# Hybrid RG-LRU and neighbourhood-attention block on one core: the second half's q and k are transposed by VectorE and fetched on ScalarE's queue, and the score maxima are ordered ahead of the gate banks

## The chip, the core and the metric

The kernel runs on one core of a Trainium2 chip. Its engines are TensorE (PE in the profile: matmuls, and PEld: their weight loads), VectorE (DVE), ScalarE (ACT), GpSimd (POOL) and SyncE (SP, which here only issues DMAs). Each engine works through its own list of instructions in a fixed order, and an instruction at the head of that list that waits holds up all that stand behind it. The metric is the device time of one execution in microseconds, the median of several runs.

## What is computed

One layer of a hybrid encoder on 512 tokens (a grid of 8 rows by 64 columns) of width 1024, in float32:

```python
x = x + 0.5 * swiglu1(rmsnorm(x))
h = rmsnorm(x)
xr, gr, q, k, v, ga, gb = split(h @ w_in)
xc = depthwise_conv(xr)
y_lru = (rglru_forward(xc) + rglru_backward(xc)) * gelu(gr)
q = rmsnorm(q, q_norm) * 64 ** -0.5          # per head, 16 heads of 64
k = rmsnorm(k, k_norm)
y_att = neighbourhood_attention(q, k, v, rel_pos_bias)
y = sigmoid(ga) * y_lru + sigmoid(gb) * y_att
x = x + y @ w_out
x = x + 0.5 * swiglu2(rmsnorm(x))
```

The attention window of a block of 16 columns is 8 rows by 32 columns, with a softmax over 256 (at the edges 192) keys and a learned bias.

## The kernel before

**Matmuls in three products.** A float32 weight tile `wraw` (128x1024, loaded by SP) is split into a rounded part `wh` and a rest `wl`: a cast on ScalarE (L138; for half of the gate and recurrence weights on VectorE, L140) and then a subtraction on VectorE (L141). Each k tile gives three matmuls into one PSUM bank: `xh*wh` (L166), `xl*wh` (L167), `xh*wl` (L168). The pool holds 3 `wraw`, 4 `wh` and 4 `wl`. So the split of a weight tile can be written only when the tile four chunks earlier has been read for the last time: `wh` after that chunk's last L167, `wl` after its last L168, which is its last matmul.

**Stages.** FFN1 comes first, then the projection `xr` with convolution and recurrence, then q, k and v in two halves of 8 heads, then the gate projections, then `w_out` and FFN2. A gate chunk is 24 matmuls of 128x512 (8 k tiles by 3) into one of the 4 `acc` banks; VectorE evicts it with a multiplication by the reciprocal norm (L1173), and ScalarE applies gelu or tanh to two chunks at once (L1177). VectorE then multiplies the result into the recurrence output A (L1187, L1190).

**Attention between the gate chunks.** Attention runs as a generator `heads()` (L991) in the lane "att". `weave` is called in the middle and at the end of each gate chunk, adds the lane's rate (0.7 in this phase) to its due count, and takes as many steps as are due; so the number of `yield`s decides between which gate chunks a step's matmuls stand. The second half handles four feature tiles (two heads each), numbered `fi` = 0 to 3 here. Its steps are:

- normalize q and k in place (L1004, VectorE),
- `start(fi)` (L1009): 8 transposes on PE (L1013 for q, L1015 for k) into two `aux` banks, then `qh` (ScalarE L1019), `ql` (VectorE L1021), `kh` (ScalarE L1022), `kl` (VectorE L1024). `start(0)` has its own step, `start(1)` to `start(3)` follow the scores before them,
- `scores(fi)` (L1028): 24 matmuls (L1045) into two `aux` and two `acc` banks, the first of which reads `kl`; then, for each of four banks, two reductions `so`/`nmx` on VectorE (L1065: bias added and maximum found, after which the bank is free), two `Exp` on ScalarE (L1072), a reciprocal (L1074) and two scalings on VectorE (L1077),
- `ship(fi)`: the probabilities are transposed on VectorE (L1086, L1087), written to DRAM by SP and fetched by GpSimd as `PT`,
- `apply(fi)`: 32 matmuls with v (L1108) two units later.

**What sets the order.** Within each engine a scheduler sorts the instructions at build time by its own estimate of when each can start; `tc.high_priority()` puts an instruction ahead of others that are ready, `after(i, prev)` forces an order, and `hold(i)` puts an instruction behind the last matmul issued so far. On the chip the order is fixed.

In what follows the gate chunks around the second half's scores are named by their place. In the changed kernel scores(0) stands between chunks 7 and 8, scores(1) between 9 and 10, scores(2) within chunk 11 and scores(3) between 12 and 13. Chunk 7 fills bank `acc_5425`, chunk 8 `acc_5594`, chunk 9 `acc_5626`, chunk 10 `acc_5759`, chunk 12 `acc_5975`.

## Time and profile before

| what | value |
|---|---|
| median of 3 runs | 1082.92 us (1082.89 to 1083.47) |
| profiled execution | 1082.5 us, of which the span is 1080.7 us |
| stage | us from the span's start |
| FFN1 | 0 to 344 |
| xr, convolution, recurrence | 344 to 395 |
| q, k, v in two halves, first gate work | 395 to 546 |
| gate chunks with attention | 546 to 705 |
| w_out | 705 to 752 |
| FFN2 | 752 to 1081 |

In the rows of groups, `out<-in` are the program's tile names; then come the count, the busy time and the mean duration of one in ns, and last the idle time of the engine just ahead of these instructions with what ended it. Rows of a timeline hold the start, the duration, the engine, the line and what is written from what; the durations of neighbours on one engine overlap a little, so a step is read from start to start.

### The profile page before, as it was taken

The numbers are of one execution on the slowest core, as the hardware profiler recorded it, in microseconds if no ns is written. First come the engines' busy times: TensorE is split into PE (matmuls) and PEld (weight loads), VectorE is DVE, ScalarE is ACT, GpSimd is POOL, SyncE is SP. The second block draws the span as 40 slices with busy tenths as digits, with TensorE's granted clock in tenths as the row PEclk, the third lists the DMA queues.
The fourth block names the chain that finished last, engine by engine and source line by source line (L and its number), as shares of the span: only waits on it lengthen the run. The fifth ranks groups of instructions, "written<-read, shape, count | busy, mean of one in ns | idle before, by whom it ended". The sixth has DMA issues, their size and how long they took to land.

```text
span 1080.7 us, 14413 instructions
## 1 busy us (share of the span) xinstructions
PE 1075.3 (99%) x5121; PEld 883.1 (82%) x5121; DVE 770.5 (71%) x1222; ACT 561.6 (52%) x867; POOL 197.8 (18%) x340
## 2 busy tenths in 40 slices
PE   9999999999999999999999999999999999999998
PEld 7888888888888778788877888888888888888887
DVE  7799778774327876999868986758687787764322
ACT  8755555553215778877354642456455555543320
POOL 0110002431000441330345232000001001332000
PEclk9999999999999999999999999999999999999999
DMA  9879675974324685573777576665476777676222
GB/s 356 182 228 246 180 192 135 248 250 148 98 83 146 194 231 155 169 212 104 229 235 219 170 242 205 192 223 160 97 188 188 187 210 167 184 241 198 93 71 79
DMA packets 67464, 198.18 MB, mean 183 GB/s; under 512 B 11072, under 2 KB 12864, under 8 KB 67392
## 3 DMA queue, kind: packets, MB, share of 16 engines
q1 hardware_dynamic: 46736, 136.66, 37.6%
q0 software_dynamic: 20512, 60.34, 25.0%
q8 instruction: 40, 0.66, 0.2%
q14 instruction: 32, 0.26, 0.1%
q10 hardware_dynamic: 144, 0.26, 0.1%
HBM read 162.06 MB, written 26.74 MB: 175 GB/s over the span
## 4 chain that ended last, share of the span: by engine, by line
PE 96%; DVE 2%; DMA 1%; ACT 1%; issue 0%; SPq 0%; ACTq 0%; DVEq 0%
PE acc L318 20%; PE aux L318 15%; PE acc L166 10%; PE acc L168 10%; PE acc L167 10%; PE acc L926 4%; PE acc L927 4%; PE acc L928 4%; PE aux L168 4%; PE aux L166 4%; PE aux L167 4%; PE aux L493 2%; PE aux L1108 1%; PE aux L837 1%; DMA vd<-v 1%; PE aux L1045 1%
## 5 line engine op out<-in xcount | busy, mean ns | idle before, releaser
L141 DVE TENSOR_TENSOR wl<-wraw,wh 128x1024 fp32r<-128x1024 f32 (+2 forms) x147 | 168.9, 1150 | 153.4 <-ACT wh L138 153.0
L138 ACT ACTIVATE wh<-wraw 128x1024 fp32r<-128x1024 f32 (+2 forms) x135 | 134.5, 998 | 224.6 <-PE acc L167 158.2
L141 DVE TENSOR_TENSOR wl<-pair,wh 128x1024 fp32r<-128x1024 f32 x80 | 97.6, 1223 | 42.2 <-ACT wh L138 41.9
L138 ACT ACTIVATE wh<-pair 128x1024 fp32r<-128x1024 f32 x80 | 84.7, 1061 | 77.5 <-PE aux L318 47.8
L166 PE MATMUL acc<-xh,wh 128*128 128x512 f32 x288 | 114.0, 396 | 0.0
L168 PE MATMUL acc<-xh,wl 128*128 128x512 f32 x288 | 112.6, 391 | 0.0
L167 PE MATMUL acc<-xl,wh 128*128 128x512 f32 x288 | 112.5, 391 | 0.0
L318 PE MATMUL aux<-wh,s 128*128 128x512 f32 x320 | 98.5, 389 | 0.0
L318 PE MATMUL acc<-wh,s 128*128 128x512 f32 x320 | 98.5, 389 | 0.0
L926 PE MATMUL acc<-wh,xh 128*128 128x512 f32 x192 | 75.7, 394 | 0.0
L927 PE MATMUL acc<-wh,xl 128*128 128x512 f32 x192 | 74.8, 389 | 0.0
L928 PE MATMUL acc<-wl,xh 128*128 128x512 f32 x192 | 74.7, 389 | 0.0
L318 PEld LDWEIGHTS acc<-wh,s 128*128 128x128 f32 x320 | 60.1, 188 | 12.5
L318 PEld LDWEIGHTS aux<-wh,s 128*128 128x128 f32 x320 | 60.1, 188 | 12.5
L167 PE MATMUL aux<-hl,wh 128*128 128x512 f32 (+1 forms) x179 | 69.3, 387 | 0.0
L168 PE MATMUL aux<-hh,wl 128*128 128x512 f32 (+1 forms) x179 | 69.3, 387 | 0.0
L166 PE MATMUL aux<-hh,wh 128*128 128x512 f32 (+1 forms) x179 | 69.0, 387 | 0.0
L168 PE MATMUL acc<-hh,wl 128*128 128x512 f32 (+1 forms) x176 | 68.1, 387 | 0.0
L167 PE MATMUL acc<-hl,wh 128*128 128x512 f32 (+1 forms) x176 | 68.1, 387 | 0.0
L166 PE MATMUL acc<-hh,wh 128*128 128x512 f32 (+1 forms) x176 | 68.0, 387 | 0.0
L166 PEld LDWEIGHTS acc<-xh,wh 128*128 128x128 f32 x288 | 54.1, 188 | 13.0 <-issue 2.3
L168 PEld LDWEIGHTS acc<-xh,wl 128*128 128x128 f32 x288 | 54.1, 188 | 11.5 <-issue 0.4
(230 smaller groups left out, 2412.3 us busy)
## 6 DMA issues: line engine op xcount, KB each, us to landing
wraw<-wqkv SPq DMA_DIRECT2D x24, 512.0 KB, 4.7
...
```

The source lines that it names most:

```text
L138: mark["H"] = nc.scalar.activation(H, raw, AF.Copy)
L141: mark["L"] = nc.vector.tensor_tensor(L, raw, H.bitcast(F32), ALU.subtract)
L166: nc.tensor.matmul(ps, wh, xh, start=first, stop=False, skip_group_check=skip)
L167: nc.tensor.matmul(ps, wh, xl, start=False, stop=False, skip_group_check=skip)
L168: mark["mm"] = nc.tensor.matmul(ps, wl, xh, start=False, stop=last, skip_group_check=skip)
L318: mark["mm"] = nc.tensor.matmul(pss[tb], x_[:, s], w_[:, c], start=first and k == 0 and x_ is xh_ and w_ is H, stop=k == 3 and w_ is L, sk ...
L493: mark["mm"] = nc.tensor.matmul(pre[tb], x_[:, tb * P : (tb + 1) * P], w_, start=k == 0 and x_ is xh[k] and w_ is H, stop=k == KT - 1 and ...
L837: prev, mm = mm, nc.tensor.matmul(ps[d][b], W[w][o, c], X[x][o], start=x == 1, stop=w + x == 0)
L926: nc.tensor.matmul(pss[j], xh[kk][:, tj], H[:, s], start=kk == 0, stop=False)
L927: nc.tensor.matmul(pss[j], xl[kk][:, tj], H[:, s], start=False, stop=False)
L928: mark["mm"] = nc.tensor.matmul(pss[j], xh[kk][:, tj], L[:, s], start=False, stop=kk == KT - 1)
L1045: mm = hold(nc.tensor.matmul(ps[hp][:, cs], q_[o, n * P : (n + 1) * P], keys(k_[o]), start=k_ is kl, stop=q_ is ql))
```

## The change

Six things are changed, most of them in the attention's second half.

1. The 32 transposes of q and k on PE in the second half go. Instead 8 VectorE transposes (32x32 blocks, one for q and one for k in each of four token blocks) write 128x1024 tiles `pair`, 4 DMAs of 512 KB on SP's queue bring these to DRAM (`qd`), and 4 DMAs per feature tile on ScalarE's queue (`fetch`, 16 in all) fetch them as `xqk`, of which there is one buffer. `qh`, `ql`, `kh` and `kl` then read `xqk` in SBUF instead of PSUM banks. Normalizing is now a generator of its own in a lane "prep"; the factor `k_norm` is folded into q's factor `gq8`.
2. In the second half the scaling of the probabilities (16 instructions on 128x256 and 16 on 128x192) moves from VectorE to ScalarE.
3. All gate weights are cast on ScalarE; before, 12 of the 24 were cast on VectorE.
4. The eviction of a gate chunk is ordered after the last score reduction written so far (`after(e, mark["so"])`).
5. The bias tiles are loaded earlier and with priority.
6. There is one more step ahead of the second half's first scores, and the fetches of later tiles stand in the loop. Buffers are moved about to make room (`big` has 40 instead of 42).

Shown as diff, each hunk without its outer context:

```diff
@@ -78,8 +78,8 @@
     "t0": {"att": 0.0, "lru": 3.25},
-    "t1": {"att": 0.75, "tail": 0.75, "lru": 2},
-    "g": {"att": 0.7, "tail": 0.7, "lru": 1.5, "v": 0.5},
+    "t1": {"att": 0.75, "tail": 0.75, "lru": 2, "prep": 1.0},
+    "g": {"att": 0.7, "tail": 0.7, "lru": 1.5, "v": 0.5, "prep": 1.0},
 }
@@ -104,7 +104,7 @@
 
-    NBIG = 42
+    NBIG = 40
@@ -658,8 +658,8 @@
 
-    lanes = {"att": [], "tail": [], "lru": [], "v": []}
-    due = {"att": 0.0, "tail": 0.0, "lru": 0.0, "v": 0.0}
+    lanes = {"att": [], "tail": [], "lru": [], "v": [], "prep": []}
+    due = {"att": 0.0, "tail": 0.0, "lru": 0.0, "v": 0.0, "prep": 0.0}
@@ -773,7 +773,7 @@
     after(nc.vector.tensor_scalar(gq8, small[:, C_QN : C_QN + 1], HD**-0.5, None, ALU.mult), mark["h"])
-    gk = small[:, C_KN : C_KN + 1]
+    nc.vector.tensor_tensor(gq8, gq8, small[:, C_KN : C_KN + 1], ALU.mult)
@@ -857,7 +857,10 @@
             hold(nc.vector.tensor_tensor(ix, ix, xc[f], ALU.mult))
-            th = big_t(n="th")
+            if d == 1 and f < 3:
+                th = big.tile([P, T], F32, name=nm("th"), **(dict(tag="xqk", bufs=1) if f == 0 else dict(tag="PT", bufs=5)))
+            else:
+                th = big_t(n="th")
             act("tanh", nc.scalar.activation(th, r, AF.Tanh, scale=sp4[:, f * 2 + d : f * 2 + d + 1]))
@@ -938,7 +941,7 @@
         for j, t in enumerate(raws):
-            sq = big_t(n="sq")
+            sq = big.tile([P, T], F32, tag="pt", bufs=2, name=nm("sq"))
             after(nc.scalar.activation(sq, t, AF.Square), copy)
@@ -984,11 +987,12 @@
             bms[g, hp] = tiny.tile([P, 640], F32, tag="bm", bufs=4, name=nm("bm"))
-            ld = nc.gpsimd.dma_start(bms[g, hp], a["rpb"][g * 2 + hp])
+            with tc.high_priority():
+                ld = nc.gpsimd.dma_start(bms[g, hp], a["rpb"][g * 2 + hp])
             if g == 0:
                 after(ld, mark["xr"])
 
-    def heads(hf, raws, st):
+    def norm_qk(raws, st, qd):
@@ -998,30 +1002,68 @@
         yield
-        for w in range(2):
-            for j in range(NCB):
+        out = []
+        for j in range(NCB):
+            for w in range(2):
                 t = raws[w][j].rearrange("p (h d) -> p h d", d=HD)
                 hold(nc.vector.tensor_tensor(t, t, rq[:, w, j, :].unsqueeze(2).to_broadcast([P, 8, HD]), ALU.mult))
+            if qd is not None:
+                t2 = pair_t().rearrange("p a b -> p (a b)")
+                for w in range(2):
+                    nc.vector.transpose(
+                        t2.rearrange("p (c f w i) -> p w f c i", c=NCB, f=4, w=2)[:, w],
+                        raws[w][j].rearrange("p (f c i) -> p f c i", c=NCB, i=32))
+                while out:
+                    hold(nc.sync.dma_start(*out.pop()))
+                out.append((qd[j], t2))
+                yield
+            elif j % 2 == 1:
+                yield
+        if qd is not None:
+            hold(nc.sync.dma_start(*out.pop()))
             yield
+            yield
+            fetch(qd, 0)
+
+    xs = {}
+
+    def fetch(qd, fi):
+        t = xs[fi] = big.tile([P, NCB * NCB, 2, 32], F32, tag="xqk", bufs=1, name=nm("xqk"))
+        for c in range(NCB):
+            hold(nc.scalar.dma_start(
+                t[c * 32 : (c + 1) * 32].rearrange("p g w i -> p g (w i)"),
+                qd.rearrange("j (a i) c f x -> c f i (j a) x", a=NCB)[c, fi]))
+
+    def heads(hf, raws, qd):
+
+        if hf == 1:
+            until("prep", lambda: False)
         qk, rss, soft, PTs = {}, {}, {}, {}
 
 
         def start(fi):
-            fs = slice(fi * P, (fi + 1) * P)
-            pq, pk = aux_t(), aux_t()
-            for j in range(NCB):
-                hold(nc.tensor.transpose(pq[:, j * P : (j + 1) * P], raws[0][j][:, fs], ident))
-            for j in range(NCB):
-                hold(nc.tensor.transpose(perm(pk)[:, j], raws[1][j][:, fs], ident))
             rev = lambda t: t.rearrange("p (j t) -> p j t", j=NCB)[:, :, ::-1]
-            fwd = lambda t: t.rearrange("p (j t) -> p j t", j=NCB)
+            if hf == 0:
+                fs = slice(fi * P, (fi + 1) * P)
+                pq, pk = aux_t(), aux_t()
+                for j in range(NCB):
+                    hold(nc.tensor.transpose(pq[:, j * P : (j + 1) * P], raws[0][j][:, fs], ident))
+                for j in range(NCB):
+                    hold(nc.tensor.transpose(perm(pk)[:, j], raws[1][j][:, fs], ident))
+                xq, xk = pq.rearrange("p (j t) -> p j t", j=NCB), pk
+                q_of, k_of = rev, lambda t: t
+            else:
+                x = xs.pop(fi).rearrange("p (j a) w i -> p w j a i", j=NCB)
+                xq, xk = x[:, 0], x[:, 1].rearrange("p j a (r c) -> p j a r c", r=2)
+                q_of = lambda t: rev(t).rearrange("p j (a i) -> p j a i", i=32)
+                k_of = lambda t: t.rearrange("p (a r j c) -> p j a r c", a=NCB, r=2, j=NCB)
             qh, ql, kh, kl = (big_t(F32R, n=n) for n in ("qh", "ql", "kh", "kl"))
-            nc.scalar.activation(rev(qh), fwd(pq), AF.Copy, scale=gq8)
+            hold(nc.scalar.activation(q_of(qh), xq, AF.Copy, scale=gq8))
             with tc.high_priority():
-                nc.vector.scalar_tensor_tensor(rev(ql), fwd(pq), gq8, rev(qh.bitcast(F32)), ALU.mult, ALU.subtract)
-            nc.scalar.activation(kh, pk, AF.Copy, scale=gk)
+                nc.vector.scalar_tensor_tensor(q_of(ql), xq, gq8, q_of(qh.bitcast(F32)), ALU.mult, ALU.subtract)
+            hold(nc.scalar.activation(k_of(kh), xk, AF.Copy))
             with tc.high_priority():
-                mark["kl"] = nc.vector.scalar_tensor_tensor(kl, pk, gk, kh.bitcast(F32), ALU.mult, ALU.subtract)
+                mark["kl"] = nc.vector.tensor_tensor(k_of(kl), xk, k_of(kh.bitcast(F32)), ALU.subtract)
             grid = lambda t: t.rearrange("p (r c) -> p r c", r=ROWS)
@@ -1062,7 +1104,7 @@
                     with tc.high_priority():
-                        nc.vector.tensor_tensor_reduce(
+                        mark["so"] = nc.vector.tensor_tensor_reduce(
                             so_, ps[hp][:, o : o + w], bm[:, BIAS[n]],
@@ -1074,7 +1116,10 @@
                     n = n2 * 2 + i
-                    nc.vector.tensor_scalar(pt, pt, rs[:, hp, n : n + 1], None, ALU.mult)
+                    if hf == 0:
+                        nc.vector.tensor_scalar(pt, pt, rs[:, hp, n : n + 1], None, ALU.mult)
+                    else:
+                        nc.scalar.activation(pt, pt, AF.Copy, scale=rs[:, hp, n : n + 1])
             return mm
@@ -1125,9 +1170,13 @@
         if hf == 1:
+            fetch(qd, 1)
+            yield
             yield
         LC = ATT_LAG[hf]
         for i, (fi, n2s) in enumerate(units):
+            if 0 in n2s and hf * 4 + fi + 1 < KT:
+                bias(hf * 4 + fi + 1)
             behind = scores(fi, n2s)
@@ -1136,11 +1185,11 @@
                     start(fi + 1)
-                if hf * 4 + fi + 1 < KT:
-                    bias(hf * 4 + fi + 1)
             if phase[0] == "g":
                 yield
                 if hf == 1:
+                    if fi < 2:
+                        fetch(qd, fi + 2)
                     yield
@@ -1159,8 +1208,13 @@
         raws = [qk_raw(0, hf, st), qk_raw(1, hf, st)]
+        if hf == 1:
+            qd = dram.tile([NCB, P, NCB, 4, 64], F32, name="qd")
+            lanes["prep"].append(norm_qk(raws, st, qd))
         v_get(hf)
-        lanes["att"].append(heads(hf, raws, st))
+        if hf == 0:
+            lanes["att"].append(norm_qk(raws, st, None))
+        lanes["att"].append(heads(hf, raws, qd if hf == 1 else None))
         phase[0] = "t1" if hf == 0 else "g"
@@ -1168,9 +1222,11 @@
             ps = acc_t()
-            feat_chunk(a["wg3"][w * KT + f], KT, xh, xl, ps, 0, KT, f % 2 == 0, RATE[phase[0]])
+            feat_chunk(a["wg3"][w * KT + f], KT, xh, xl, ps, 0, KT, True, RATE[phase[0]])
             with tc.high_priority():
-                nc.vector.tensor_tensor(q[i // 2][:, i % 2], ps, rb, ALU.mult)
+                e = nc.vector.tensor_tensor(q[i // 2][:, i % 2], ps, rb, ALU.mult)
+                if "so" in mark:
+                    after(e, mark["so"])
             weave(RATE[phase[0]])
```

What that does to the order of the engines is shown at two places. The first is VectorE around the second half's scores(0). Before, from the last `kl` ahead of scores(0) to the first reductions of its scores (`wl` is a weight split, `A` the product with the recurrence, `pair` a gate eviction):

```order
L1024 SCALAR_TENSOR_TENSOR kl_5421<-aux_5409,small,kh_5420 128x512
L141 TENSOR_TENSOR wl_5810<-wraw_5808,wh_5809 128x1024
L1187 TENSOR_TENSOR A_5460<-pair_5260,th_3687 128x512
L1187 TENSOR_TENSOR A_5462<-pair_5260,th_3735 128x512
L1187 TENSOR_TENSOR A_5464<-pair_5261,th_4144 128x512
L1187 TENSOR_TENSOR A_5466<-pair_5261,th_4194 128x512
L1173 TENSOR_TENSOR pair_5468<-acc_5470,rstd_2948 128x512
L141 TENSOR_TENSOR wl_5850<-wraw_5848,wh_5849 128x1024
L1065 ISA so_5535,nmx_5536<-aux_5503,bm_5130 128x192
```

In the changed kernel, VectorE just ahead of scores(0), and then, four rows further on, among the reductions of its scores:

```order
L141 TENSOR_TENSOR wl_5818<-wraw_5816,wh_5817 128x1024
L1243 TENSOR_TENSOR A_5298<-pair_4964,th_3514 128x512
L1243 TENSOR_TENSOR A_5300<-pair_4964,th_3594 128x512
L1063 SCALAR_TENSOR_TENSOR ql_5359<-xqk_5103,gq_2899,qh_5358 128x4x128
L1066 TENSOR_TENSOR kl_5361<-xqk_5103,kh_5360 128x4x8x16
L1107 ISA so_5481,nmx_5482<-aux_5449,bm_5127 128x192
```

```order
L141 TENSOR_TENSOR wl_5978<-wraw_5976,wh_5977 128x1024
L1107 ISA so_5490,nmx_5491<-aux_5450,bm_5129 128x192
L1107 ISA nmx_5491 128x1
L1107 ISA so_5490,nmx_5491<-aux_5450,bm_5129 128x256
L1107 ISA nmx_5491 128x1
L1107 ISA so_5499,nmx_5500<-acc_5451,bm_5127 128x256
```

The split `wl_5818` now stands four rows ahead of `kl_5361`, which the first matmul of scores(0) reads; before, `kl_5421` was followed by a split, not preceded by it. And `wl_5978` stands within the reductions, ahead of `so_5499`, which frees bank `acc_5451`; before, an eviction (L1173) stood ahead of the split and freed a bank there.

The second place is ScalarE around the second half's `kh` of feature tile 1, before:

```order
L1019 ACTIVATE qh_5601<-aux_5591,gq_2899 128x4x128
L1072 ACTIVATE p_5534,rs_5502<-so_5562,nmx_5563 128x256
L1072 ACTIVATE p_5533,rs_5502<-so_5562,nmx_5563 128x192
L1022 ACTIVATE kh_5603<-aux_5592,small 128x512
L1177 ACTIVATE pair_5468<-pair_5468 128x1024
L1118 ACTIVATE att_5681<-aux_5664 128x512
L138 ACTIVATE wh_6043<-wraw_6042 128x1024
```

and in the changed kernel from the weight cast ahead of scores(0) on, and then from the gelu of the gates to the same `kh` (`kh_5539`):

```order
L138 ACTIVATE wh_5817<-wraw_5816 128x1024
L1061 ACTIVATE qh_5358<-xqk_5103,gq_2899 128x4x128
L1064 ACTIVATE kh_5360<-xqk_5103 128x4x8x16
L1033 DMA xqk_5379<-qd 32x16x64 x4
L138 ACTIVATE wh_5977<-wraw_5976 128x1024
L1114 ACT_TABLE_LOAD
L1114 ACTIVATE p_5477,rs_5448<-so_5481,nmx_5482 128x192
```

```order
L1233 ACTIVATE pair_5303<-pair_5303 128x1024
L1122 ACTIVATE p_5480<-p_5480,rs_5448 128x256
L1122 ACTIVATE p_5479<-p_5479,rs_5448 128x192
L1122 ACTIVATE p_5480<-p_5480,rs_5448 128x256
L138 ACTIVATE wh_6009<-wraw_6008 128x1024
L1122 ACTIVATE p_5479<-p_5479,rs_5448 128x192
L1064 ACTIVATE kh_5539<-xqk_5379 128x4x8x16
```

Here `wh_5817`, `wh_5977` and `wh_6009` are casts for the splits above. The cast now stands ahead of `qh` and `kh`, while before the cast `wh_6043` came behind `kh`. Between the two pieces ScalarE has the `Exp`s, four scalings (L1122) and `qh_5537`. The bank that chunk 9 fills is the one that `so_5499` frees, chunk 11 that of `so_5700`, chunk 13 that of `so_5889`; the splits `wl_6150` and `wl_6222` stand in the same place among the reductions of scores(1) and of scores(2). `wl_6010` stands directly ahead of `kl_5540` on VectorE, the tile that scores(1) waits for.

## The prediction

> **What bounds the kernel.** I read the page's busy shares first, then the chain that ended last, then what PE waited for.
>
> ```profile
> PE 1075.3 (99%) x5121; PEld 883.1 (82%) x5121; DVE 770.5 (71%) x1222; ACT 561.6 (52%) x867; POOL 197.8 (18%) x340
> PEclk9999999999999999999999999999999999999999
> ...
> PE 96%; DVE 2%; DMA 1%; ACT 1%; issue 0%; SPq 0%; ACTq 0%; DVEq 0%
> ```
>
> PE is busy 99% of the span at a granted clock of full speed in every slice, and the chain that ended last runs over PE for 96%. The view of waits says what the missing per cent is: it lists three waits.
>
> ```profile
> PE aux L132 <- DVE pol L762: 1.1, 1, 1.1
> PE aux L1108 <- DVE ql L1021: 0.4, 1, 0.4
> PE aux L493 <- ACT xh L192: 0.3, 1, 0.3
> ```
>
> They sum to 1.8 us in 1080.7. The table by stretches gives the stretch in which the second half's attention lies:
>
> ```profile
> 590.00:705.00 115.00, 115.00 (x715) 94.74 (x711) 91.37 (x214) 49.88 (x107) 24.25 (x42) 1.00 0.65 200
> ```
>
> PE is busy for all of its 115.00 us, VectorE for 91.37 and ScalarE for 49.88. So work taken off VectorE, or put on ScalarE, is worth nothing by itself here. The time moves only in two ways: PE has less to do, or PE starts to wait. PE's reserve against waiting is the order in the other engines' lists, and two rows show how thin it can be:
>
> ```profile
> L141 DVE TENSOR_TENSOR wl<-wraw,wh 128x1024 fp32r<-128x1024 f32 x132 | 161.0, 1220 | 153.4 <-ACT wh L138 153.0
> L138 ACT ACTIVATE wh<-wraw 128x1024 fp32r<-128x1024 f32 x120 | 127.1, 1059 | 222.8 <-PE acc L167 157.6 <-issue 29.2 <-PE acc L927 18.0
> ```
>
> 120 casts waited 157.6 us in all for a chunk's last L167, and the 132 subtractions 153.0 us for their casts. A split is therefore written as soon as a finished chunk frees its buffers, hardly earlier, and it is late in the sense that whatever stands behind it in ScalarE's or VectorE's list can't run before that chunk has ended. That does no harm as long as PE's next instructions need nothing that stands behind it.
>
> **What the change removes from PE.** 32 transposes in four starts. The first start stands among matmuls:
>
> ```profile
> 587.67 0.40 PE L166 MATMUL acc<-xh,wh 128*128 128x512 f32 x1
> 588.27 0.40 PE L168 MATMUL acc<-xh,wl 128*128 128x512 f32 x1
> ...
> 591.72 0.50 PE L166 MATMUL acc<-xh,wh 128*128 128x512 f32 x1
> ```
>
> ```profile
> 599.64 0.28 PE L1045 MATMUL acc<-kh,ql 64*128 64x256 f32 x2
> ...
> 600.70 0.48 PE L166 MATMUL acc<-xh,wh 128*128 128x512 f32 x1
> ```
>
> ```profile
> 608.30 0.39 PE L166 MATMUL acc<-xh,wh 128*128 128x512 f32 x1
> 608.75 0.39 PE L168 MATMUL acc<-xh,wl 128*128 128x512 f32 x1
> 610.97 0.50 PE L166 MATMUL acc<-xh,wh 128*128 128x512 f32 x1
> ...
> 647.20 0.28 PE L1045 MATMUL acc<-kh,ql 64*128 64x256 f32 x2
> 647.41 0.44 PE L1108 MATMUL aux<-PT,va 128*64 128x128 f32 x4
> ```
>
> Three starts come in a block behind scores: from the last L1045 to the next L166 are 600.70-599.64 = 1.06 us, and without a start 647.41-647.20 = 0.21 us, so 0.85 us each, 2.55 us. The first start: from 588.27 to 591.72 are 3.45 us for the last matmul, four k transposes and an `apply`, which without transposes took 610.97-608.75 = 2.22 us: 1.23 us (with VectorE's 0.4 us wait in it). The four q transposes ahead of it stand singly among matmuls: with one of them the two steps from 587.67 to 588.27 take 0.60 us, without one 608.75-608.30 = 0.45, so 0.15 us each, 0.6 us. **Sum: 2.55 + 1.23 + 0.6 = 4.4 us gained.**
>
> **What it moves, place by place.** A chunk's matmuls follow each other by (608.75-608.30)/2 = 0.225 us, a chunk takes 24 x 0.225 = 5.4 us. The order shows seven places at which PE now needs something that stands behind a split whose buffer the chunk directly before frees, or behind the work that follows such a split.
>
> *A, scores(0) after chunk 7.* VectorE has `wl_5818`, two products A, `ql_5359`, `kl_5361` in this order, and `kl` is read by the first matmul. The cast starts just before the chunk's end:
>
> ```profile
> 613.79 1.06 ACT L138 ACTIVATE wh<-wraw 128x1024 fp32r<-128x1024 f32 x1 [2.05 <-PE acc L167]
> 613.91 0.39 PE L1045 MATMUL aux<-kl,qh 64*128 64x256 f32 x2
> ```
>
> ```profile
> 598.11 1.06 ACT L138 ACTIVATE wh<-wraw 128x1024 fp32r<-128x1024 f32 x1 [2.13 <-issue]
> ```
>
> ```profile
> 596.80 1.29 DVE L1187 TENSOR_TENSOR A<-pair,th 128x512 f32<-128x512 f32 x2
> 599.20 1.23 DVE L141 TENSOR_TENSOR wl<-wraw,wh 128x1024 fp32r<-128x1024 f32 x1 [0.22 <-ACT wh L138]
> 600.35 0.35 DVE L1065 CUSTOM_DVE_ANT_0 so<-aux,bm 128x192 f32<-128x192 f32 x1
> 600.97 0.08 DVE L1065 DVE_READ_ACCUMULATOR2_ANT nmx<- 128x1 f32 x1
> 604.51 0.74 DVE L1021 SCALAR_TENSOR_TENSOR ql<-aux,gq,qh 128x512 fp32r<-128x512 f32 x1
> 605.17 0.21 DVE L1074 RECIPROCAL rs<-rs 128x2 f32<-128x2 f32 x2
> ```
>
> Count from the moment at which the scores would start. The cast starts at 613.79-613.91 = -0.12; the subtraction follows the cast's start by 599.20-598.11 = 1.09, at 0.97; what stands behind it by 600.35-599.20 = 1.15, at 2.12; two products take 1.24 (the 1.29 less an overlap of 0.05), to 3.36; `ql` 605.17-604.51 = 0.66, to 4.02. Then `kl`:
>
> ```profile
> L1024 DVE SCALAR_TENSOR_TENSOR kl<-aux,small,kh 128x512 fp32r<-128x512 f32 x8 | 5.9, 740 | 0.0
> ```
>
> 0.74, to 4.76. **A = 4.8 us.** `qh` and `kh` on ScalarE stand behind the cast and end by 0.97 + 2 x 0.67 = 2.3, in time for neither to add.
>
> *B, D and F, chunks 9, 11 and 13.* The bank of each is freed by the third pair of score reductions, and four reductions stand behind a split that waits for the end of the chunk directly before. So 2.12 for the split, then twice a 192 and a 256 reduction at 600.97-600.35 = 0.62, 1.24 together, and about 0.1 for the last one's end: **3.5 us each.** That is what the order "score maxima ahead of the gates' banks" costs here: before, an eviction ahead of the split freed a bank.
>
> *C, scores(1) after chunk 9.* `kl_5540` stands directly behind `wl_6010`, and `wh_6009` on ScalarE behind a backlog. The pieces:
>
> ```profile
> L1072 ACT ACTIVATE p<-so,nmx 128x256 f32<-128x256 f32 x32 | 15.9, 498 | 11.3 <-DVE nmx L1065 7.7 <-DMA vd<-v 3.5
> L1177 ACT ACTIVATE pair<-pair 128x1024 f32<-128x1024 f32 x11 | 11.7, 1061 | 26.1 <-DVE pair L1173 26.1
> L1077 DVE TENSOR_SCALAR p<-p,rs 128x256 f32<-128x256 f32 x32 | 11.4, 355 | 0.1
> L1072 ACT ACT_TABLE_LOAD x4 | 5.1, 1283 | 2.3 <-DVE nmx L1065 2.2
> L1022 ACT ACTIVATE kh<-aux,small 128x512 fp32r<-128x512 f32 x8 | 5.4, 675 | 3.4 <-PE aux L1015 3.4
> ```
>
> Count from chunk 8's end: `wh_5977` to 0.94, the table load 1.28 to 2.2, five `Exp`s at 0.46 (their start to start) to 4.5, four scalings to 6.1, one `Exp`, `qh`, two `Exp`s (0.45 + 0.6 + 0.9) to 8.1, table load and gelu (1.28 + 1.06) to 10.4, three scalings to 11.6, `wh_6009` to 12.7, `wl_6010` 1.15 to 13.8, `kl` 0.74 to 14.6. PE is there at 3.5 (B) + 5.4 = 8.9, so **C = 5.7 us**; without the backlog it would be 2.12 + 0.74 = 2.9. ScalarE's scaling isn't in the trace: I bound it by VectorE's 355 ns and the `Exp` at 498 ns on the same tile and take 0.4, which leaves C between 5.4 and 6.4 (seven scalings).
>
> *E, scores(2) within chunk 11.* No cast stands between here, but the same backlog does: up to the two `Exp`s 8.1, gelu 1.06, `kh` 0.67, `kl` 0.74 make 10.6 from chunk 10's end; PE is there at 3.5 (D) + 20 x 0.225 = 8.0. **E = 2.6**, between 0 and 3.6.
>
> *G, scores(3) after chunk 12.* Counted in the same way, with an attention copy and four scalings ahead of `kh` and no table load: about 11.0, against 3.5 (F) + 5.4 = 8.9. **G = 2.1**, between 0 and 3.
>
> **What costs nothing.** VectorE loses work:
>
> ```profile
> L140 DVE CAST wh<-wraw 128x1024 fp32r<-128x1024 f32 x12 | 8.3, 692 | 8.2 <-PE acc L167 7.2 <-PE acc L927 1.0
> L1087 DVE STREAM_TRANSPOSE pt<-p 128x512 f32<-128x512 f32 x16 | 11.0, 689 | 0.0
> ```
>
> 12 casts at 692 ns go to ScalarE at 1059 ns, 12.7 us more on an engine that is free for 65 of 115 us; cover gone, it is what C counts. The 8 new transposes have the duration of L1087 and lie in the steps ahead of scores(0). The 4 writes of 512 KB join SP's queue behind weight loads that are three tiles ahead; I put 0 to 3 us on them, and take 0. For the fetches the nearest row is
>
> ```profile
> PT<-pd POOLq DMA_DIRECT2D x64, 112.0 KB, 4.3
> ```
>
> A fetch is 4 such transfers, and stands about a chunk and an apply ahead of its `qh`: I take 0, and up to 2 us a tile, 8 us, if four queue up. There is one `xqk`, so a fetch waits on ScalarE's queue until `kl` of the tile before is read; behind it stands a cast that waits for a chunk's end anyway. The extra bias priority, the buffers moved and the one `tensor_tensor` for `kl` instead of the fused form lie beside PE: 0.
>
> **Sum.** 4.8 + 3 x 3.5 + 5.7 + 2.6 + 2.1 = 25.7 us lost, 4.4 gained: 1082.5 - 4.4 + 25.7 = 1103.8 us by the profiled execution's own time. That execution lies 0.4 us below the median of 1082.92, so against the median I forecast **1104.2 us**, 2.0% slower. What is firm in it are the places where nothing but the split stands between (A, B, D, F and 2.9 of C): 18.2 us, 1096.7.
>
> [...]
>
> **The rivals.**
>
> *Faster: the splits have slack.* If the pools hand a split buffers that an older chunk freed, it is written a chunk (5.4 us) before PE's need. It decides from a slack of 5.7 us, the largest of the seven; E and G have their cover then too, and only the transposes count: 1082.92 - 4.4 = 1078.5. For it: before, too, splits stand ahead of reductions without a wait. Against it: the casts' 157.6 us of waiting for L167, and only 4 buffers. Chance 0.10.
>
> *One side only.* If the bank evictions go early enough, so that the change doesn't do what its words say about the maxima, A, C, E and G stay: 15.2 us, 1093.7. If `kl` is early instead, B, D and F stay: 10.5, 1089.0. For the first: four `acc` banks are a reserve. Chance 0.13 together.
>
> *More: PE slow after a pause, or late fetches.* If PE runs the half chunk after each of five pauses (A to D, F) at half pace, 12 x 0.225 = 2.7 us each, 13.5 us come on top: 1117.7. Late fetches give up to 8 us, 1112. For it: pauses of a new kind, and 256-byte pieces. Against it: a granted clock of 1.00 everywhere, and fetches a chunk ahead. Chance 0.18.
>
> *No change:* the gain and small stalls cancel, which needs just 4.4 us of stalls: 0.03.
>
> **How the numbers follow.** The forecast with its firm part, 1096 to 1110, has 0.53; the remaining 0.03 lie between the cases above no change. A measurement of this kernel tells about 0.2%, 2.2 us, from no change. The range reaches from the bank-side case to the upper rival, 1088 to 1117, and leaves out 0.10 + 0.03 below and some 0.07 of the upper rival and the rest. Faster 0.10, within 0.2% 0.03, slower 0.87.
>
> **What would show it.** PE's waits after should list scores (L1087) behind `kl`, three or four times, some 15 us, and the first matmul of a chunk (L166) behind `nmx` three times with about 3.5 us each. The stretch that holds scores would show PE's busy share down by about a fifth of 115 us, with granted clock 1.00. L1013 and L1015 should count 16 instead of 32. It would be wrong if these waits are absent, if they are ended by a DMA into `xqk`, or if the matmuls behind them run slower.

## The result, and the profile after

The changed kernel takes 1106.7 us (median of 6 runs, 1105.84 to 1107.32) beside 1082.91 us of the kernel before on the same chip: the ratio is 1.0218, with a 95% interval of 1.0205 to 1.0232. The forecast was 1104.2 us. The profiled execution took 1106.16 us with a span of 1104.1 us, 23.4 us more than before.

What PE waited for in the changed kernel, the two new rows (columns: us in all, how often, the longest):

```profile
PE acc L166 <- DVE rs L1116: 10.5, 3, 3.5
PE aux L1087 <- DVE kl L1066: 7.9, 3, 4.7
```

That is 10.5 us for the first matmul of a chunk (L166) and 7.9 us for scores (L1087). The releaser of the first, `rs` of L1116, is the reciprocal that stands directly behind the fourth of the reductions. On the page, PE's busy time has grown from 1075.3 to 1080.7 us although 32 transposes are gone:

```profile
PE 1080.7 (98%) x5089; PEld 886.9 (80%) x5089; DVE 759.1 (69%) x1187; ACT 588.0 (53%) x913; POOL 196.9 (18%) x340
```

The granted clock shows why. The stretch that holds scores, and in it the first 3.4 us of chunk 9 and what follows scores(1)'s start (after the busy times of the five engines comes the granted clock, here 0.91, 0.50 and 0.72):

```profile
590.00:705.00 115.00, 98.06 (x591) 79.28 (x592) 62.63 (x152) 58.75 (x133) 29.19 (x50) 0.91 0.67 191
607.00:610.40 3.40, 3.20 (x8) 2.56 (x9) 1.24 (x8) 3.40 (x13) 0.58 (x1) 0.50 0.71 237
618.50:622.00 3.50, 3.46 (x28) 2.97 (x29) 3.47 (x9) 0.00 (x0) 0.07 (x1) 0.72 0.94 220
```

Before, PE was busy for all 115.00 us of that stretch at a clock of 1.00; now it is busy for 98.06 us at 0.91. Behind five of its six pauses the clock was 0.50: behind chunk 9's, matmuls followed each other by 0.43 us (607.76 to 612.88), and by 0.23 us once it was 1.00 again (613.28 to 615.37). The pauses one by one, in PE's timeline (the number in brackets is the idle time ahead of the row, and what ended it):

```profile
593.12 0.58 PE L1087 MATMUL aux<-kl,qh 64*128 64x256 f32 x2 [4.70 <-DVE kl L1066]
607.20 0.77 PE L166 MATMUL acc<-xh,wh 128*128 128x512 f32 x1 [3.52 <-DVE rs L1116]
618.53 0.39 PE L1087 MATMUL aux<-kl,qh 64*128 64x256 f32 x2 [2.77 <-DVE kl L1066]
633.16 0.47 PE L166 MATMUL acc<-xh,wh 128*128 128x512 f32 x1 [3.51 <-DVE rs L1116]
640.00 0.38 PE L1087 MATMUL aux<-kl,qh 64*128 64x256 f32 x2 [0.46 <-DVE kl L1066]
653.76 0.47 PE L166 MATMUL acc<-xh,wh 128*128 128x512 f32 x1 [3.51 <-DVE rs L1116]
```

They stand where the forecast put them: scores(0), chunk 9, scores(1), chunk 11, scores(2), chunk 13. scores(3) does not wait.

The sum of the traces: the waits are 18.4 us where 0.4 us of the same kind stood before, 18.0 more; PE's busy time is 5.4 us more; together the 23.4 us of the spans. The kernel `e11_repaired_both` below gives the split of the 5.4: with the same matmuls and no such pause it has 1071.3 us of busy time, so the transposes gave 4.0 us and the slow clock took 1080.7-1071.3 = 9.4 us. This split is good to about 1 us: `e9_repaired_scaling_on_vector`, which has no such pause either, has 1072.2 us.

The two causes read like this, first the cast on ScalarE and VectorE ahead of scores(0), then VectorE among the reductions ahead of chunk 9:

```profile
588.28 1.06 ACT L138 ACTIVATE wh<-wraw 128x1024 fp32r<-128x1024 f32 x1 [0.84 <-ACT pair L1233]
...
589.38 1.21 DVE L141 TENSOR_TENSOR wl<-wraw,wh 128x1024 fp32r<-128x1024 f32 x1
590.51 1.28 DVE L1243 TENSOR_TENSOR A<-pair,th 128x512 f32<-128x512 f32 x2
591.72 0.74 DVE L1063 SCALAR_TENSOR_TENSOR ql<-xqk,gq,qh 128x512 fp32r<-128x512 f32 x1
592.38 0.68 DVE L1066 TENSOR_TENSOR kl<-xqk,kh 128x512 fp32r<-128x512 f32 x1
...
604.58 1.22 DVE L141 TENSOR_TENSOR wl<-wraw,wh 128x1024 fp32r<-128x1024 f32 x1 [9.07 <-ACT wh L138]
...
606.69 0.08 DVE L1107 DVE_READ_ACCUMULATOR2_ANT nmx<- 128x1 f32 x1
```

The cast starts 0.14 us ahead of chunk 7's end at 593.12-4.70 = 588.42, where the working said 0.12 (the gelu that its row names had ended at 587.4). Then come `wl` (L141), the products A (L1243), `ql` (L1063), `kl` (L1066), and PE starts at 593.12. In the second piece `wl` follows its cast at 604.58, only then come the reductions (L1107), and PE starts at 607.20.

### The profile page after: what moved, and what is told of

Read it like the earlier page. It is cut to its first block, busy times and chain, and to the rows that moved or that the text cites. A ratio compares the mean times of both kernels' runs of the same rounds, so it can differ in the third digit from the quotient of the medians.

```text
span 1104.1 us, 14408 instructions
## 1 busy us (share of the span) xinstructions
PE 1080.7 (98%) x5089; PEld 886.9 (80%) x5089; DVE 759.1 (69%) x1187; ACT 588.0 (53%) x913; POOL 196.9 (18%) x340
## 4 chain that ended last, share of the span: by engine, by line
PE 94%; DVE 2%; ACT 2%; DMA 1%; issue 1%; SPq 0%; DVEq 0%; ACTq 0%; POOLq 0%
PE acc L318 20%; PE aux L318 15%; PE acc L166 10%; PE acc L167 10%; PE acc L168 10%; PE acc L929 4%; PE acc L930 4%; PE acc L931 4%; PE aux L166 4%; PE aux L167 4%; PE aux L168 4%; PE aux L493 2%; PE aux L1153 1%; PE aux L837 1%; PE aux L1087 1%
## 5 line engine op out<-in xcount | busy, mean ns | idle before, releaser
L141 DVE TENSOR_TENSOR wl<-wraw,wh 128x1024 fp32r<-128x1024 f32 (+2 forms) x147 | 168.9, 1150 | 186.5 <-ACT wh L138 183.6
L138 ACT ACTIVATE wh<-wraw 128x1024 fp32r<-128x1024 f32 (+2 forms) x147 | 147.2, 1003 | 275.3 <-PE acc L167 198.4
L166 PE MATMUL acc<-xh,wh 128*128 128x512 f32 x288 | 117.4, 408 | 10.5 <-DVE rs L1116 10.5
L141 DVE TENSOR_TENSOR wl<-pair,wh 128x1024 fp32r<-128x1024 f32 x80 | 97.4, 1221 | 42.2 <-ACT wh L138 42.0
L168 PE MATMUL acc<-xh,wl 128*128 128x512 f32 x288 | 115.4, 401 | 0.0
L167 PE MATMUL acc<-xl,wh 128*128 128x512 f32 x288 | 115.0, 399 | 0.0
L166 PEld LDWEIGHTS acc<-xh,wh 128*128 128x128 f32 x288 | 55.9, 194 | 25.6 <-issue 14.0
L167 PE MATMUL aux<-hl,wh 128*128 128x512 f32 (+1 forms) x179 | 69.3, 387 | 0.0
L166 PE MATMUL aux<-hh,wh 128*128 128x512 f32 (+1 forms) x179 | 69.0, 387 | 0.0
L167 PE MATMUL acc<-hl,wh 128*128 128x512 f32 (+1 forms) x176 | 68.1, 387 | 0.0
L166 PE MATMUL acc<-hh,wh 128*128 128x512 f32 (+1 forms) x176 | 68.0, 387 | 0.0
```

Source lines behind the costliest of these rows:

```text
L138: mark["H"] = nc.scalar.activation(H, raw, AF.Copy)
L141: mark["L"] = nc.vector.tensor_tensor(L, raw, H.bitcast(F32), ALU.subtract)
L166: nc.tensor.matmul(ps, wh, xh, start=first, stop=False, skip_group_check=skip)
L167: nc.tensor.matmul(ps, wh, xl, start=False, stop=False, skip_group_check=skip)
L168: mark["mm"] = nc.tensor.matmul(ps, wl, xh, start=False, stop=last, skip_group_check=skip)
```

## The experiments

The theory: a weight split waits for the chunk directly before and stands in VectorE's and ScalarE's lists ahead of what PE needs next, and the pauses bring the stretches at a clock of 0.50 with them. The rivals: ScalarE carries too much (the scalings and 12 casts moved there), the way of q and k through DRAM is late, or the order of the evictions alone does it.

### Edges that put the splits last

The first three runs change nothing but the order. Edges are added behind the changed kernel's casts (`wh`) and subtractions (`wl`) of gate weights; `bound` holds the `kh` and `kl` of the scores that stand behind each chunk, `maxima` the last reduction ahead of it.

```diff
         with tc.high_priority():
             split(raw[:, s], H[:, s], L[:, s], act)
+        for i in first["wh"]:
+            after(mark["H"], i)
+        for i in first["wl"]:
+            after(mark["L"], i)
...
+            n = len(bound) - 4
+            m = n + 1
+            first["wh"] = [bound[m][0]] if 0 <= m < len(bound) and bound[m] else []
+            first["wl"] = [bound[m][1]] if 0 <= m < len(bound) and bound[m] else []
+            first["wl"] += [maxima[n]] if n >= 0 and maxima[n] else []
+            maxima.append(mark.get("so"))
             feat_chunk(a["wg3"][w * KT + f], KT, xh, xl, ps, 0, KT, True, RATE[phase[0]])
```

The second run has `n` in place of `m`; the third has that and no `maxima`.

> The changed kernel with ordering edges only: each gate weight's cast and subtraction stand behind the kh and kl of the scores one chunk after the chunk that frees their buffers, and the subtraction behind the score maxima ahead of that chunk. Nothing else is changed. Theory (the splits stand ahead of kl and of the maxima): no wait of the first matmul of a chunk on the reductions and no wait of scores on kl above 1 us, granted clock 1.00 between 546 and 705, and only the removed transposes count: 1078.5 us, ratio to before 0.996. Rival (ScalarE carries too much, 28 us more): kl and the banks stay late, PE waits of 15 us or more, 1098 or above. Rival (the fetch through DRAM lands late): scores wait for kl 5 us or more, ended by the DMA into xqk, 1085 or above.

Measured: 1088.0 us (1085.72 to 1091.5), ratio 1.0046 (1.0031 to 1.0060). PE's waits on attention in the profiled run, the fastest of the six:

```profile
PE aux L1095 <- DVE kl L1071: 6.5, 3, 3.3
```

The waits of chunks are gone, scores(1)'s stays at 2.7 and scores(0)'s at 3.3. So an order of the splits alone takes back 18.7 of the 23.8 us, and the theory in its pure form is refuted: something else holds `kl` too. VectorE ahead of scores(0) in this run:

```profile
588.47 1.85 DVE L1261 TENSOR_TENSOR A<-pair,th 128x512 f32<-128x512 f32 x3
590.24 0.75 DVE L1068 SCALAR_TENSOR_TENSOR ql<-xqk,gq,qh 128x512 fp32r<-128x512 f32 x1
```

No split stands here any more. VectorE works without a gap from 582.89 to 591.5: on the first half's probabilities (L1128, L1139, L1140), then on the products A (L1261, the last three in one row), and only then on `ql` and `kl` (L1068, L1071). `qh` and `kh` were written by 587.5. So a split stood in the way in the changed kernel, but VectorE's backlog alone comes to within 1.5 us of the same end. At scores(1) the cause is another: the fetch is late here. ScalarE in this run:

```profile
591.62 1.94 ACTq L1038 DMA_DIRECT2D xqk<-qd  x4
...
603.64 0.73 ACT L1066 ACTIVATE qh<-xqk,gq 128x512 fp32r<-128x512 f32 x1 [4.36 <-DMA xqk<-qd]
```

ScalarE's queue (ACTq) issues the four DMAs of tile 1 from 591.62 on, as soon as `kl` of tile 0 has read the one buffer. `qh` starts 12.0 us after the first issue and keeps ScalarE idle for 4.36 us, and `kh` and `kl` of scores(1) stand behind it. That is more than PE's wait of 2.7, so the rival of the late fetch is partly right in this run, although PE's wait is put down to `kl` and not to a DMA.

> The same edges, but the cast and the subtraction stand only behind the kh and kl of the scores directly behind the chunk that frees their buffers; so on ScalarE one cast still stands ahead of all Exp of the scores before it and waits for the chunk behind those scores. Theory: the waits at scores(0) (4.7) and at chunks 9, 11 and 13 (3.5 each) go, and ScalarE's backlog, which starts at that cast, now shows alone: kl of scores(1) is done about 13.3 us after chunk 8's end, PE is there after 5.4, so about 7.9; scores(2) about 6, scores(3) up to 5.6; 14 to 20 us of waits, and with a slower clock after them 1092 to 1106 us. If the splits on VectorE alone were the cause, PE would not wait at all: 1078.5.

Measured: 1108.34 us (1107.17 to 1108.71), ratio 1.0233 (1.0218 to 1.0248). PE's four pauses:

```profile
593.15 0.58 PE L1095 MATMUL aux<-kl,qh 64*128 64x256 f32 x2 [4.82 <-DVE kl L1071]
617.11 0.58 PE L1095 MATMUL aux<-kl,qh 64*128 64x256 f32 x2 [8.02 <-DVE kl L1071]
639.99 0.58 PE L1095 MATMUL aux<-kl,qh 64*128 64x256 f32 x2 [5.84 <-DVE kl L1071]
661.03 0.58 PE L1095 MATMUL aux<-kl,qh 64*128 64x256 f32 x2 [3.99 <-DVE kl L1071]
```

scores(0) still waits 4.82 us, which was not expected and has the cause named for it in the run before, VectorE's backlog; it puts the time above the stated range. The rest came as forecast: no wait of a chunk, and 8.02, 5.84 and 3.99 us at scores(1) to scores(3) against 7.9, 6 and up to 5.6. One cast on ScalarE that waits for a chunk's end, ahead of all `Exp`, delays the whole chain of probabilities that `kh` stands behind. The total is no better than the changed kernel's: of the waits, those of chunks went and those of scores took their place.

> The edges for kh and kl as in the run before, without those for the maxima. Theory: scores(0) no longer waits (4.7 gone, and the slow matmuls behind that pause), chunks 9, 11 and 13 wait 3.5 us each as before, scores(1) 1 to 4.4 and scores(2) 0 to 2.3 by ScalarE's backlog; about 1099 us, between 1096 and 1102. Rival (bank waits are only another face of late kl): they go with it, 1085 or below.

Measured: 1104.27 us (1103.85 to 1104.74), ratio 1.0194 (1.0181 to 1.0207). Waits:

```profile
PE acc L171 <- DVE rs L1124: 10.5, 3, 3.5
PE aux L1095 <- DVE kl L1071: 6.9, 4, 3.6
```

The three waits of 3.5 us stay to the hundredth, so they hang on the split among the reductions and on nothing that late `kl` does; the rival falls. The time missed the stated 1096 to 1102, again because scores(0) keeps 3.56 us.

### Undoing one part at a time

```diff
                 e = nc.vector.tensor_tensor(q[i // 2][:, i % 2], ps, rb, ALU.mult)
-                if "so" in mark:
-                    after(e, mark["so"])
```

> The changed kernel without the ordering of a gate eviction behind the score maxima; everything else as changed. Theory: the waits of chunks 9, 11 and 13 go (10.5), but the eviction of the chunk directly before scores(1) to scores(3), and a weight split behind it, now stand ahead of the reductions that kl follows, so these scores wait instead: about 2.9 at scores(0), 7.6, 6.5 and 7.5 at the others, 24 in all, with a slower clock behind each; 1105 to 1114 us, no gain from the undoing. Rival (the ordering alone costs the bank waits and the slow matmuls behind them): scores wait as before, 7.9 in all, and 1089 to 1096 us.

Measured: 1110.63 us (1110.06 to 1111.71), ratio 1.0252 (1.0238 to 1.0266).

```profile
PE aux L1087 <- DVE kl L1066: 25.8, 4, 8.1
```

The four waits are 3.4, 7.8, 6.5 and 8.1 us (expected 2.9, 7.6, 6.5 and 7.5). Score maxima behind the gates' evictions cost more than ahead of them. The edge in the change does not cause the loss by itself; it moves it from scores to banks.

```diff
-                    if hf == 0:
-                        nc.vector.tensor_scalar(pt, pt, rs[:, hp, n : n + 1], None, ALU.mult)
-                    else:
-                        nc.scalar.activation(pt, pt, AF.Copy, scale=rs[:, hp, n : n + 1])
+                    nc.vector.tensor_scalar(pt, pt, rs[:, hp, n : n + 1], None, ALU.mult)
```

> The changed kernel with the second half's probabilities scaled on VectorE as before; everything else as changed. Theory (the order of the splits decides, ScalarE's load only adds to it): 4.7 at scores(0) and three times 3.5 at chunks 9, 11 and 13 stay, the 2.8 at scores(1) and 0.5 at scores(2) go; 1102 to 1105 us. Rival (ScalarE's load is the cause): most waits go, below 1090 us.

Measured: 1101.34 us (1099.55 to 1101.8), ratio 1.0162 (1.0148 to 1.0176).

```profile
PE acc L166 <- DVE rs L1116: 10.5, 3, 3.5
PE aux L1087 <- DVE kl L1066: 5.5, 3, 4.7
```

Of the 5.5 us 4.7 are scores(0)'s. The waits of the order stay and scores(1)'s shrinks to 0.5, so the kernel gains about 5 us of the 23.8 by it, a little more than expected. This is not the price of the scalings alone: with them gone from ScalarE's list, the split that stood ahead of scores(1)'s `kl` came to stand behind it (`wl` starts at 619.10, `kl` at 614.46). The scalings are not the main cause.

```diff
-            feat_chunk(a["wg3"][w * KT + f], KT, xh, xl, ps, 0, KT, True, RATE[phase[0]])
+            feat_chunk(a["wg3"][w * KT + f], KT, xh, xl, ps, 0, KT, f % 2 == 0, RATE[phase[0]])
```

> The changed kernel with 12 of the 24 gate weight casts on VectorE again; everything else as changed. Theory: the three waits of 3.5 at chunks 9, 11 and 13 or, where the cast is on VectorE, about 0.4 less or more each, and 3 to 5 at scores(0) stay; 1100 to 1110 us. Rival (the casts on ScalarE are the cause): below 1090 us.

Measured: 1105.87 us (1103.9 to 1109.09), ratio 1.0210 (1.0193 to 1.0227): no difference to the changed kernel's 1.0218. In the profiled run, the slowest of the four, the banks wait 10.5 us behind the reductions as before and once 1.3 us behind an eviction; scores(0) waits 5.5, a little more than stated. The way through DRAM, the bias tiles and the buffers (parts 1, 5 and 6 of the change) were not undone by themselves.

### A pause by itself

The kernel before, with chains of memsets of a spare tile that PE has to wait for between chunks of `w_out` (3, 6 and 9 of them; in the second run 1, 2 and 3).

```diff
+        for i in range(PAUSE.get(m, 0)):
+            p = nc.gpsimd.memset(scratch, 0.0)
+            if i == 0:
+                after(p, mark["mm"], sync=True)
+            pause[0] = p
         feat_chunk(a["wout"][m], KT, yh, yl, ps, 0, KT)
...
-        nc.tensor.matmul(ps, wh, xh, start=first, stop=False, skip_group_check=skip)
+        mm = nc.tensor.matmul(ps, wh, xh, start=first, stop=False, skip_group_check=skip)
+        if pause[0] is not None:
+            after(mm, pause[0], sync=True)
```

> The kernel before, with three pauses of PE put between chunks of w_out by chains of 3, 6 and 9 GpSimd memsets of a spare tile, about 1.8, 3.4 and 5.1 us long, and nothing else. Theory (a pause itself slows PE behind it): granted clock below 1.00 behind the pauses, behind the longer ones surely, and the matmuls behind them at up to twice the spacing for some us; the span grows by the pauses, about 10.3, and 3 to 9 us more. Rival (the slow clock in the changed kernel had another cause, such as load of the other engines): granted clock 1.00 behind all three, and the span grows by the pauses alone.

Measured in a single run: 1099.43 us, span 1097.7, 17.0 more than before. The pauses in PE's timeline, and the stretches behind them:

```profile
713.35 0.50 PE L168 MATMUL acc<-yh,wh 128*128 128x512 f32 x1 [1.81 <-POOL scratch L1219]
729.74 0.80 PE L168 MATMUL acc<-yh,wh 128*128 128x512 f32 x1 [3.61 <-POOL scratch L1219]
748.69 0.79 PE L168 MATMUL acc<-yh,wh 128*128 128x512 f32 x1 [5.36 <-POOL scratch L1219]
```

```profile
713.35:714.40 1.05, 1.05 (x5) 0.87 (x6) 1.05 (x3) 0.81 (x2) 0.00 (x0) 1.00 0.44 168
714.40:717.90 3.50, 3.50 (x10) 2.74 (x9) 0.53 (x1) 0.00 (x0) 0.00 (x0) 0.51 0.84 281
729.74:733.90 4.16, 4.16 (x10) 3.30 (x11) 0.00 (x0) 0.00 (x0) 0.00 (x0) 0.50 0.58 226
748.69:751.80 3.11, 3.11 (x7) 2.48 (x8) 1.73 (x3) 0.55 (x2) 0.00 (x0) 0.50 0.48 151
```

10.8 us are the pauses; the other 6.2 lie in the three slow stretches, in which matmuls follow each other by some 0.43 us (729.74 to 733.90 holds 10 where 0.225 us each would give 18). Behind the longer pauses the clock is 0.50 from the first matmul, behind the one of 1.81 us it is 1.00 for one more microsecond, then 0.51 for 3.5. So each of these pauses cost about 2 us on top of its length, without any of the changed kernel's load on the other engines.

> The kernel before with three short pauses of PE in w_out, by chains of 1, 2 and 3 GpSimd memsets: about 0.7, 1.2 and 1.8 us, 3.7 together. In the run with long pauses the pause of 1.81 already had a granted clock of 0.50 behind it. If a slow stretch follows from a fixed length of pause between 1 and 1.8, only the last pause is followed by one, and the time is 1082.9 + 3.7 + 1.7 = 1088.3 us. If it depends on where the pause falls, single runs differ, by about 1.7 us a slow stretch, between 1086.6 and 1092.

Measured: 1087.52 us (1086.64 to 1089.47), ratio 1.0043 (1.0027 to 1.0060). The pauses of the profiled run:

```profile
711.93 0.50 PE L168 MATMUL acc<-yh,wh 128*128 128x512 f32 x1 [0.64 <-POOL scratch L1219]
724.39 0.50 PE L168 MATMUL acc<-yh,wh 128*128 128x512 f32 x1 [1.29 <-POOL scratch L1219]
737.44 0.50 PE L168 MATMUL acc<-yh,wh 128*128 128x512 f32 x1 [1.87 <-POOL scratch L1219]
```

In that run the clock is 1.00 behind all three, also behind 1.87 us, and the span's 1084.9 us are the 1080.7 of before and the pauses' 3.8 to within 0.4. One of the four runs, 1089.47 us, has a mean clock of 0.998, the others 1.000; its cause is open, since a run of the kernel before, of 1085.74 us, shows 0.998 too. So a pause of 1.8 us was followed by a slow stretch in one trace and not in another.

The traces show more. In the changed kernel the stretches at a clock of 0.50 start at 592.76, 606.42, 620.07, 633.73 and 654.21, whole multiples of 3.41 us apart, and each lasts 3.41 us, the one at 606.42 twice that. Below, its time is cut into pieces of 3.41 us from these starts. The changed kernel's piece ahead of the first slow one, and that one:

```profile
589.35:592.76 3.41, 0.00 (x0) 0.00 (x0) 3.41 (x6) 1.11 (x2) 1.11 (x3) 1.00 0.89 258
592.76:596.17 3.41, 3.06 (x26) 2.83 (x28) 1.01 (x5) 0.00 (x0) 3.41 (x7) 0.50 1.08 278
```

And the two pieces over which the 2.69 us pause ahead of scores(1) in `e1_split_behind_both` is spread (the pieces counted from its slow stretch, which starts at 592.51):

```profile
606.16:609.57 3.41, 1.78 (x8) 1.13 (x6) 0.73 (x2) 3.40 (x7) 0.15 (x1) 1.00 0.90 228
609.57:612.98 3.41, 2.35 (x27) 2.10 (x28) 3.34 (x5) 2.50 (x5) 0.82 (x2) 1.00 0.91 294
```

No slow stretch follows these: the clock is 1.00 in both, and the matmuls behind them are 0.23 us apart (612.68 to 613.83). In the changed kernel PE was busy for 0.00, 0.68, 1.53, 0.56 and 0.44 us of the five pieces ahead of the slow stretches, and for 2.48 us or more of every other piece at full clock. In `e4_pauses_alone` the pause of 1.81 us lies wholly in the piece from 711.02 to 714.43, just ahead of the slow stretch, with 1.60 us of PE's work. So in these traces a slow stretch went not with a pause's length but with how much of one piece it took: 1.81 us that left 1.60 was followed by one, 2.69 us that left 1.78 and 2.35 was not. Where the pieces lie in the run with 1.87 us can't be read in the same way, since it has no slow stretch.

### Repairs

To the edges of the first run this kernel adds three further steps ahead of the second half's first scores, and puts the eviction of the chunk directly before scores behind their `kl`.

```diff
             fetch(qd, 1)
             yield
             yield
+            yield
+            yield
+            yield
...
                     after(e, mark["so"])
+            old = mark.get("need")
             weave(RATE[phase[0]])
+            if mark.get("need") is not old:
+                after(e, mark["need"][1])
```

> The kernel of the first run with two things more: three further steps ahead of the second half's first scores, so that they stand about a chunk and a half later and VectorE has done the first half's probabilities and the products with A by then, and the eviction of the chunk directly before scores is ordered behind the kl of these scores. Theory (what was left in the first run, 3.3 at scores(0) and 2.7 at scores(1), is VectorE's and ScalarE's backlog, not the fetch): no wait above 0.5 us, granted clock 1.00, 1078.5 us, ratio 0.996. Rival (the fetch route or ScalarE's DMA issues bind): scores still wait for kl, 3 us or more in all, and 1082 or above.

Measured: 1082.65 us (1080.21 to 1084.7), ratio 0.9991 (0.9982 to 1.0001). What was left of waits on attention in the profiled run, the fastest, of 1080.21 us:

```profile
PE aux L1161 <- DMA PT<-pd: 1.8, 1, 1.8
PE aux L1095 <- DVE kl L1071: 0.6, 1, 0.6
```

With more room ahead of them scores(0) and scores(1) no longer wait, which the theory of the backlog expected; the late fetch of the first run has more room too. The 0.6 us left for `kl`, at scores(3), are the fetch's: `qh` of that tile, at 643.10, had waited 0.56 us for the DMA into `xqk`. The median missed the expected 1078.5 and lies where the rival was put. What was not expected: an `apply` (L1161) waits 1.8 us for `PT`. Eight of the ten other runs have a mean clock of 0.998 and take 1.7 to 3.3 us more; no trace shows why.

The next three change this kernel. The first scales on VectorE (the diff is that of `e6_scaling_on_vector`), the second sets `ATT_LAG = 4, 3` in place of `4, 2`, the third has both.

> The repaired kernel (run e8_repaired) with the second half's probabilities scaled on VectorE as before the change. Theory (e8's one wait left, 1.8 us of an apply for the DMA that brings PT, comes from scalings that stand late in ScalarE's list, and in most of its runs, at clock 0.998, a slow stretch follows it): the probabilities are ready earlier, the wait goes, 1078.5 to 1080 us, ratio 0.996 to 0.998. Rival (PT's DMAs wait for other reasons, such as SP's queue): the wait stays near 1.8 and the time near 1082.6.

Measured: 1078.86 us (1078.08 to 1079.42), ratio 0.9958 (0.9946 to 0.9971). No wait of attention is left.

> The repaired kernel (run e8_repaired) with apply three units behind its scores instead of two, in the second half only. Theory: PT has a unit of scores and a chunk or two more to land, the 1.8 us wait goes, 1078.5 to 1080 us. Rival (something else made the median of e8 2.4 us longer than its profiled run): the wait goes and the time stays at 1082.6.

Measured: 1085.92 us (1084.0 to 1087.18), ratio 1.0024 (1.0015 to 1.0033). Neither came: the wait for `PT` went and a longer one came for `kl`. The same matmul here, and in the run without the later apply:

```profile
646.40 0.58 PE L1095 MATMUL aux<-kl,qh 64*128 64x256 f32 x2 [4.83 <-DVE kl L1071]
```

```profile
646.15 0.39 PE L1095 MATMUL aux<-kl,qh 64*128 64x256 f32 x2 [0.61 <-DVE kl L1071]
```

`kl` is done at 646.4 and 646.2, at the same time in both. PE only came there 4 us earlier, without an apply (2.2 us) and the wait of 1.8 ahead of it. What sets that moment is the fetch of the last tile, as ScalarE's row in the run with the later apply shows:

```profile
643.32 0.72 ACT L1066 ACTIVATE qh<-xqk,gq 128x512 fp32r<-128x512 f32 x1 [5.45 <-DMA xqk<-qd]
```

ScalarE stood idle for 5.45 us. In both runs `qh` starts 14.4 to 14.7 us after the fetch's first issue, and a wait of PE taken away ahead of it is given back there.

> The repaired kernel with both, scaling on VectorE and apply a unit later. Theory: no wait for PT and none for kl, granted clock 1.00 in all runs, 1078.5 us. Rival as above: 1082 us or more.

Measured: 1078.39 us (1078.14 to 1079.24), ratio 0.9958 (0.9944 to 0.9971), the fastest kernel here beside `e9_repaired_scaling_on_vector`, from which it can't be told. The head of its page, and the stretch:

```profile
PE 1071.3 (100%) x5089; PEld 880.4 (82%) x5089; DVE 765.6 (71%) x1219; ACT 573.8 (53%) x879; POOL 196.8 (18%) x340
```

```profile
590.00:705.00 115.00, 115.00 (x684) 94.11 (x684) 90.71 (x213) 58.77 (x118) 31.00 (x53) 1.00 0.78 234
```

PE is busy for all 115.00 us at a clock of 1.00, VectorE for 90.71. The span of 1076.4 us is 4.3 below the kernel before; by the medians beside the kernel before on the same chip, 1083.32 us, this kernel gains 4.9 and `e9_repaired_scaling_on_vector` 4.5. That is what the removed transposes are worth.

## Why the prediction held, point by point

**PE sets the time, and only waits of PE or less of its work move it: right but for a third way.** The two repaired kernels, with no wait, lose nothing by 8 more transposes on VectorE or the fetches. But the time also moves when PE runs at a lower clock, by 9.4 us here, and the prediction had granted clock 1.00 and named slower matmuls behind the waits as a sign of being wrong. That sign came.

**The gain of 4.4 us: right.** 4.3 us of span in `e11_repaired_both`, of which 4.0 are PE's busy time (good to about 1 us) and the rest the wait of 0.4 us that was counted in.

**A, scores(0), 4.8 us: right in size (4.70), half right in cause.** The split stood where it was said, but with it gone 3.3 to 4.8 us stay. What the step left out is the work of the first half that stands ahead of it on VectorE, and that the changed kernel starts these scores a chunk and an `apply` of PE's work earlier than before, since normalizing has a lane of its own (598.18 before, 593.12-4.70 = 588.42 without the wait in the changed kernel).

**B, D and F, 3.5 us each: right,** 3.52, 3.51 and 3.51. They go when the split goes from among the reductions (`e1_split_behind_both`, `e2_split_behind_kl_and_maxima`), and also when an eviction may stand ahead of it and free a bank (`e5_no_bank_order`); they stay to the hundredth in `e3_split_behind_kl_only`. So it takes the split and the order of the evictions together, as the step said.

**C, E and G: the chain was right, the size wrong.** ScalarE's part of C and its end on VectorE:

```profile
608.23 1.59 ACT L1122 ACTIVATE p<-p,rs 128x192 f32<-128x192 f32 x4
...
615.56 1.06 ACT L138 ACTIVATE wh<-wraw 128x1024 fp32r<-128x1024 f32 x1 [0.25 <-PE acc L167]
```

```profile
616.65 1.23 DVE L141 TENSOR_TENSOR wl<-wraw,wh 128x1024 fp32r<-128x1024 f32 x1 [0.59 <-ACT wh L138]
617.80 0.68 DVE L1066 TENSOR_TENSOR kl<-xqk,kh 128x512 fp32r<-128x512 f32 x1
```

Chunk 8 ends at 607.20-3.52 = 603.68, and scores(1) start at 618.53, 14.85 us later, where the working said 14.6; for scores(2) it is 640.00-(633.16-3.51) = 10.35 after chunk 10's end, where it said 10.6. scores(3), which stand behind chunk 13 and not between 12 and 13, start at 661.14, 10.89 after chunk 12's end at 653.76-3.51 = 650.25, where it said about 11.0. But PE, at a clock of 0.50 behind the pauses of B and D (from 606.42 to 613.25 and from 633.73 to 637.14), came there later: chunk 9 took about 8.5 us, not 5.4. So the waits were 2.77, 0.46 and 0 us instead of 5.7, 2.6 and 2.1. The cast at 615.56 then waited 0.25 us for chunk 9's own last L167: what is left at C is the bare split, priced at 2.9, with the backlog just hidden behind the slow chunk. In `e2_split_behind_kl_and_maxima`, where no chunk waits ahead of these scores, the same chain gave waits of 8.02 and 5.84 us where 7.9 and 6 were forecast from it. The scaling on ScalarE took 496 and 442 ns by the mean of the 256 and 192 wide ones, within the bounds, and 0.40 from start to start.

**The clock: the rival "PE slow after a pause" happened in the main case.** It took 9.4 us, where the forecast had nothing and the rival 13.5. Two terms of the sum were off, the waits by 18.4-25.7 = -7.3 us and the slow clock by +9.4, and they belong together: a slower PE waits less. That the forecast lies only 2.5 us from the result is in part luck: two errors that nearly cancel.

The rival's term, half a chunk at half pace behind each pause (2.7 us), no trace of the kernel before shows; it was the author's estimate. The runs showed the half pace, a clock of 0.50, but another length: 3.41 us, and 6.83 behind chunk 9's pause, where half a chunk at half pace would be 5.4. Pauses of 4.70 us (A), of 3.5 (B, D and F), of 2.77 (scores(1)) and once, in `e4_pauses_alone`, of 1.81 us were followed by such a stretch.

**What cost nothing: right for the changed kernel.** There no instruction waited for a DMA into `xqk`, since each `qh` came 17 us or more after its fetch's first issue. The casts changed nothing (1.0210 against 1.0218). The order of the evictions, undone, made it slower. But the fetch was priced too low, by a row of 4.3 us and up to 2 us more a tile: where `qh` came sooner it was ready only 12.0 us (`e1_split_behind_both`) and 14.7 us (`e10_repaired_apply_later`) after the first issue, and PE waited 2.7 and 4.8 us behind it. Why the fetch takes that long stays open.
